# Four expert slabs token tile by token tile, no GpSimd subtractions behind them, and transposes packed two half-chunks to a bank

## The chip, the core and the metric

The kernel runs on one core of a Trainium2 chip. The time is device microseconds of one execution from a measurement of the whole program; lower is better. The engines are TensorE (PE in the profile, its weight loads PEld), VectorE (DVE), ScalarE (ACT), GpSimd (POOL) and SyncE (SP), which issues most of the DMAs.

## The reference, cut to what matters

The program computes two blocks in float32 over 512 tokens of width 1024.

```python
def first_block(x, ...):
    xn = rmsnorm(h, mix_norm_w[l])
    proj = xn @ w_in[l]                    # then pool mixer, gated delta net, gates
    h = h + merged @ w_mix_out[l]
    h = h + peer_ffn(rmsnorm(h, ffn_norm_w[l]), ...)
    return rmsnorm(h, final_norm_w)

def peer_ffn(x, ...):                      # top 16 of 128 x 128 experts per head, 8 heads
    u = jnp.take(expert_down, ei, axis=0)
    act = gelu(einsum("btd,bthkd->bthk", xi, u))
    vv = jnp.take(expert_up, ei, axis=0)
    return einsum("bthk,bthkd->btd", gi * act, vv)

def hybrid_layer(x, norm_pre, w_in, ...):  # block 2
    h = rmsnorm_2(x, norm_pre)
    proj = einsum("bld,de->ble", h, w_in)  # then an SSD scan and stick-breaking attention
```

## The kernel before

**Tiles.** The 512 tokens are four tiles of 128. A float32 product is made of three products of numbers in a shorter format: high times high, high times low, low times high. So each weight slab (128 x 1024) is loaded by SyncE into a raw buffer (fetch), cast on ScalarE to its high half wh, and subtracted from the raw one for its low half wl (emit_part, line 263). The subtraction goes to VectorE where l_dve(i) is true, else to GpSimd. wh and wl have two buffers each. The raw buffers are raw0, raw1 and, during the expert stage, some more (xraw, hraw), which are given up near its end (from nup == NE - 11, only the raw2 list goes round). slab() takes a prepared slab, ahead() prepares the next one and fetches those behind it.

**Transposes.** Activations are turned by TensorE: feat (lines 404 to 413) returns chunk(c, tiles), which makes one transpose per token tile into a PSUM tile tp (two buffers), then split: ScalarE writes the high half (xnh, hnh or x2h), VectorE the low one (xnl, hnl, x2l) from the same PSUM tile. proj_feat calls it for eight chunks of token tiles 0 and 1, then eight chunks of tiles 2 and 3 or in another pairing (sixteen half-chunks), and puts the products of half-chunk s - 2 (first weight slab) and of s - lag (second slab) behind the transposes of half-chunk s. The products write pf. This runs at three places: the start of block 1, of the expert stage and of block 2.

**Expert stage.** 128 down slabs and 128 up slabs are multiplied densely for token tiles 1 to 3; token tile 0 gets its experts by indirect DMAs on GpSimd (gather, ringu and ringv) and sums on VectorE (hn, h_out). The pace of the second gather follows from pace2: `self.pace = (NE * 18 * 512 / 2400 - self.pace2) / (256 - self.ngather)`. An up slab is worked by up(): for t in tiles 1 to 3, six products into y1, y2, y3 (18 in all). The activations come as pairs: pair() loads them, VectorE scales them (wr), and ScalarE and VectorE split that (whl).

**The end of it.** The last two slabs go together: up(*pend, then=add) runs both slabs' tile 1, then tile 2, then tile 3, and after each calls add(t), which adds y into h_out, multiplies by the final norm's weights wf (weigh_tile, hw) and squares for the two norms (square). After the third tile norm_pair(1, 2) gives the norm of token tiles 1 and 2 and writes xs; last_norms() does tiles 0 and 3 beside the first products of block 2. The last slab is converted into the free memory of hnh (self.spare), and from nup == NE - 3 on l_dve is false: all low halves are made on GpSimd. Block 2 (block2_) starts with proj_feat over xs; its third slab is converted into a tile named third.

## Time and profile before

| | us |
|---|---|
| median of 3 runs | 2548.41 (2547.5 to 2549.49) |
| profiled execution | 2550.09 |
| its span, first to last instruction | 2548.3 |
| TensorE busy | 2459.3 (97%) |
| VectorE busy | 1709.0 (67%) |
| ScalarE busy | 994.0 (39%) |
| GpSimd busy | 656.2 (26%) |

A line of the timeline gives start and length in us, engine, line, operation, the tile written <- the tiles read, sizes, how many instructions are put together, and in brackets the idle time of the engine ahead of it and what ended it. A line of windows gives a stretch, its length, the busy time of each engine with instruction counts, the granted TensorE clock (1.00 is 2.4 GHz, 0.50 is 1.2 GHz), the DMA engines' share and GB/s. The page's section 5 groups instructions by line and tile: busy us and mean ns of one, then the idle time ahead of the group and what ended it. All stages are on one clock: block 1 to about 530, the expert stage to 1797.6, block 2 after that.

### The profile page before, as it was taken

To read this page: it belongs to the slowest core of one execution; us is meant where nothing else is said; L and a number is where in the kernel's file an instruction comes from. 1 tells how busy PE (TensorE), PEld (TensorE's weight loads), DVE (VectorE), ACT (ScalarE), POOL (GpSimd) and SP (SyncE) were. 2 spreads that over 40 slices of the span, in tenths; PEclk is the share of its full clock that TensorE was granted. 3 is DMA by queue.
4 is the path that set the end of the run, shared out by engine and by line. 5 is a ranking of instruction groups with operands and counts; after the bars stand their busy time and mean duration, and the time that the engine had idled before them with its cause. 6 is when DMAs were issued, how large, how long until landed. Compare 5 with 4: busy or idle time off the path is not lost.

```text
span 2548.3 us, 34826 instructions
## 1 busy us (share of the span) xinstructions
PE 2459.3 (97%) x13497; PEld 2108.3 (83%) x13497; DVE 1709.0 (67%) x3123; ACT 994.0 (39%) x1453; POOL 656.2 (26%) x401
## 2 busy tenths in 40 slices
PE   6999999989989999999999999999799999999997
PEld 5888788888989999999888888888678988776787
DVE  6776776558998988987577777777754430455433
ACT  4532522332245546455333333333432342444432
POOL 0000000014652222322232323322335234311142
PEclk9999999999999999999999999999899999999999
DMA  3231231324778989889999999998222123222122
GB/s 116 73 93 59 77 110 50 125 101 131 245 269 295 339 286 346 317 315 360 347 326 345 334 343 340 338 323 276 78 67 67 59 91 99 78 60 63 50 91 92
DMA packets 184982, 482.41 MB, mean 189 GB/s; under 512 B 26992, under 2 KB 77296, under 8 KB 184816
## 3 DMA queue, kind: packets, MB, share of 16 engines
q1 hardware_dynamic: 143856, 342.80, 39.5%
q0 software_dynamic: 36864, 134.23, 14.6%
q10 hardware_dynamic: 4096, 3.15, 0.6%
q8 instruction: 106, 1.74, 0.3%
q14 instruction: 60, 0.49, 0.1%
HBM read 422.45 MB, written 53.48 MB: 187 GB/s over the span
## 4 chain that ended last, share of the span: by engine, by line
PE 86%; DVE 11%; issue 2%; ACT 1%; DMA 1%; POOL 0%; SPq 0%; ACTq 0%; DVEq 0%; POOLq 0%
PE pf L175 27%; PE y L175 20%; PE pa L175 18%; PE pt L175 7%; PE psb L175 5%; DVE hn L74 3%; PE pg L175 2%; DVE wl L74 1%; PE tp L180 1%; PE pd L175 1%; PE pyd L175 1%; PE pz L175 1%; DVE oh L74 1%; DVE rt L74 0%; DVE h_out L74 0%
## 5 line engine op out<-in xcount | busy, mean ns | idle before, releaser
L74 ACT CAST wh<-raw 128x1024 fp32r<-128x1024 f32 x310 | 326.4, 1053 | 681.1 <-PE pf L175 303.3
L273 POOL TENSOR_TENSOR wl<-raw,wh 128x1024 fp32r<-128x1024 f32 x113 | 275.9, 2442 | 1047.7 <-ACT wh L74 1029.2
L175 PE MATMUL y<-wh,whl 128*128 128x512 f32 x1524 | 418.0, 395 | 3.9 <-ACT whl L74 3.9
L74 DVE TENSOR_TENSOR wl<-raw,wh 128x1024 fp32r<-128x1024 f32 x197 | 240.9, 1224 | 181.7 <-ACT wh L74 181.6
L175 PE MATMUL pa<-hnh,wl 128*128 128x384 f32 x1024 | 345.2, 337 | 11.0 <-DVE wl L74 5.5
L175 PE MATMUL pa<-hnh,wh 128*128 128x384 f32 x1024 | 347.6, 340 | 3.1 <-ACT st L74 3.1
L175 PEld LDWEIGHTS y<-wh,whl 128*128 128x128 f32 x1524 | 287.4, 189 | 72.3 <-ACT whl L74 4.3
L175 PE MATMUL pa<-hnl,wh 128*128 128x384 f32 x1024 | 343.4, 335 | 0.0
L1480 POOL DMA_INDIRECT ringv<-up,eid x128 | 171.1, 1337 | 422.6 <-DVE h_out L74 388.1
L1480 POOL DMA_INDIRECT ringu<-down,eid x128 | 156.3, 1221 | 355.4 <-DVE hn L74 335.2
L175 PE MATMUL y<-wl,whl 128*128 128x512 f32 x762 | 240.3, 396 | 0.0
L175 PEld LDWEIGHTS pa<-hnh,wl 128*128 128x128 f32 x1024 | 192.7, 188 | 15.7 <-DVE wl L74 7.8
L175 PEld LDWEIGHTS pa<-hnh,wh 128*128 128x128 f32 x1024 | 192.7, 188 | 3.5 <-ACT st L74 3.4
L175 PEld LDWEIGHTS pa<-hnl,wh 128*128 128x128 f32 x1024 | 192.8, 188 | 0.0
L175 PE MATMUL pf<-xnh,wh 128*128 128x512 f32 (+1 forms) x432 | 176.3, 409 | 2.6 <-DVE cy L74 1.7
L74 DVE SCALAR_TENSOR_TENSOR hn<-ringu,hn 128x1024 f32<-128x1024 f32 x128 | 175.0, 1367 | 0.0
L175 PEld LDWEIGHTS y<-wl,whl 128*128 128x128 f32 x762 | 143.6, 189 | 34.7 <-DVE wl L74 0.7
L175 PE MATMUL pf<-x2h,wh 128*128 128x512 f32 (+1 forms) x424 | 169.1, 399 | 2.9 <-DVE cy L74 1.2
L175 PE MATMUL pf<-xnh,wl 128*128 128x512 f32 (+1 forms) x432 | 167.8, 388 | 0.0
L74 DVE SCALAR_TENSOR_TENSOR h_out<-ringv,wgt,h_out 128x1024 f32<-128x1024 f32 x128 | 166.6, 1301 | 0.0
L175 PE MATMUL pf<-xnl,wh 128*128 128x512 f32 (+1 forms) x432 | 166.2, 385 | 0.0
L175 PE MATMUL pf<-x2h,wl 128*128 128x512 f32 (+1 forms) x424 | 166.0, 391 | 0.0
(464 smaller groups left out, 4799.6 us busy)
## 6 DMA issues: line engine op xcount, KB each, us to landing
raw<-w_in_t SPq DMA_DIRECT2D x104, 512.0 KB
raw<-down_t SPq DMA_DIRECT2D x82, 512.0 KB
raw<-up_t SPq DMA_DIRECT2D x55, 512.0 KB
hn<-up_t SPq DMA_DIRECT2D x49, 512.0 KB
Ad<-st SPq DMA_DIRECT2D x32, 768.0 KB
Gd<-stg SPq DMA_DIRECT2D x48, 512.0 KB
ar<-Ad SPq DMA_DIRECT2D x32, 768.0 KB
gr<-Gd SPq DMA_DIRECT2D x32, 768.0 KB
```

The source lines that it names most:

```text
L74: return f(*args, **kw)
L175: self.nc.tensor.matmul(ps, l, r, **kw)
L180: self.nc.tensor.transpose(ps, src, ident)
L273: low = lambda: eng.tensor_tensor(l, raw, h.bitcast(F32), OP.subtract)
L1480: nc.gpsimd.indirect_dma_start(out=(ru, rv)[kind][:, s % 4, :], out_offset=None, in_=a[("down", "up")[kind]], in_offset=bass.IndirectOffse ...
```

## The change

It has four parts.

- The last four up slabs (124 to 127) go through up() together, tile by tile; slabs 126 and 127 are converted into hnh. With four slabs there are places between the slabs of the third tile, and add(2, j) uses them: at the first one it converts block 2's first slab, runs norm_pair(1, 2) and only then the slab's low half, at the second one it converts the second slab.
- l_dve stays true to the end, and weigh_tile always runs on VectorE.
- feat puts the transposes of two half-chunks into one PSUM tile tp of shape [128, 4, 128], a new one for every second half-chunk.
- pace2 goes from 1 to 17.

```diff
-        self.pace, self.pace2, self.gpace = 4.2, 1.0, 4.0
+        self.pace, self.pace2, self.gpace = 4.2, 17.0, 4.0
...
-        if self.spare:
-            (h, l), self.spare = self.spare, None
+        if i in self.spare:
+            h, l = self.spare.pop(i)
...
-            ps = (pool or self.pmm).tile([128, 512], F32, name=self.nm("tp"), tag="tp", bufs=2)
-            for t in tiles:
-                self.tr(ps[:, t * 128:(t + 1) * 128], src[:, t, c * 128:(c + 1) * 128], self.ident)
+            n = len(tiles)
+            if c * n % NT == 0:
+                self.tps = (pool or self.pmm).tile([128, NT, 128], F32, name=self.nm("tp"), tag="tp", bufs=2)
+            o = c * n % NT
+            ps = self.tps[:, o:o + n]
+            for j, t in enumerate(tiles):
+                self.tr(ps[:, j], src[:, t, c * 128:(c + 1) * 128], self.ident)
...
                         if t == 2 and j < n - 1:
-                            self.part(self.cur + 1)
+                            then(t, j)
...
-                if self.nup == NE - 3:
+                if self.nup == NE - 4:
...
-                    self.l_dve = lambda i: False
...
-            for i in range(0, NE - 2, 2):
+            for i in range(0, NE - 4, 2):
                 two, pend = pend, pair(i + 2)
                 up(two[0])
-                if i == NE - 4:
-
-                    self.spare = [hnh[:, 2 * k:2 * k + 2, :].rearrange("p c t -> p (c t)") for k in range(2)]
-                    self.part(self.cur + 2)
+                if i == NE - 6:
+
+                    for j in range(2):
+                        self.spare[self.cur + 3 + j] = [hnh[:, 4 * j + 2 * k:4 * j + 2 * k + 2, :].rearrange("p c t -> p (c t)")
+                                                        for k in range(2)]
+                    self.part(self.cur + 3)
                 up(two[1])
-            self.part(self.cur + 2)
+            self.part(self.cur + 3)
+            last = pend + pair(NE - 2)
             self.drain(gather[0])
...
-            self.weigh_tile(0, nc.gpsimd)
-
+            self.weigh_tile(0)
             self.square(0, 0)
 
-            def add(t):
+            def add(t, j=None):
+
+                if j == 0:
+                    self.late_low = []
+                    self.part(self.cur)
+                    self.all(self.norm_pair(1, 2))
+                    for low in self.late_low:
+                        low()
+                    self.late_low = None
+                elif j == 1:
+                    self.part(self.cur + 1)
+                if j is not None:
+                    return
...
-                self.weigh_tile(t + 1, nc.gpsimd if t == 2 else nc.vector)
+                self.weigh_tile(t + 1)
...
-                    self.all(self.norm_pair(1, 2))
                     self.prep = [self.last_norms()]
-            up(*pend, then=add)
+            up(*last, then=add)
...
-            self.spare = third[:, 0], third[:, 1]
+            self.spare[self.cur + 2] = third[:, 0], third[:, 1]
```

ScalarE at the last expert slabs. Before (raw0 and raw1 are the two raw buffers, hnh is the spare memory for the last slab, whl the split activations):

```order
L74 CAST wh_1704_14851<-raw0_65 128x1024 [waits DMAHW0_49,PE_49,Activation_49]
L74 CAST wh_1706_14876<-raw1_66 128x1024 [waits DMAHW1_49,PE_49,Activation_49]
L74 CAST whl_1709_14882<-wr_1708_14881 128x768 [waits DVE_49]
L74 CAST wh_1710_14905<-raw0_65 128x1024 [waits DMAHW2_49,PE_49,Activation_49]
L74 CAST hnh_4444<-raw1_66 128x1024 [waits DMAHW3_49]
L74 CAST wh_1712_14933<-raw0_65 128x1024 [waits DMAHW4_49,PE_49,Activation_49]
L74 ACTIVATE xs_14939,ss2_67<-h_out_3649 128x1024 [waits DMASW4_49,DMASW2_49,DMASW6_49,DMASW0_49,DVE_49]
```

After, from slab 122 on:

```order
L74 CAST wh_1682_14787<-raw0_65 128x1024 [waits DMAHW4_49,PE_49,Activation_49]
L74 CAST wh_1684_14811<-raw1_66 128x1024 [waits DMAHW7_49,PE_49,Activation_49]
L74 CAST whl_1687_14817<-wr_1686_14816 128x768 [waits DVE_49]
L74 CAST wh_1688_14840<-raw0_65 128x1024 [waits DMAHW0_49,PE_49,Activation_49]
L74 CAST hnh_4436<-raw0_65 128x1024 [waits DMAHW2_49]
L74 CAST wh_1690_14865<-raw1_66 128x1024 [waits DMAHW1_49,PE_49,Activation_49]
L74 CAST hnh_4436<-raw0_65 128x1024 [waits DMAHW3_49]
L74 CAST whl_1693_14875<-wr_1692_14874 128x768 [waits DVE_49]
```

Slabs 126 and 127 are both cast into hnh, from raw0, around the cast of slab 125 from raw1, and the activations of slabs 126 and 127 (the last whl) come behind all four casts.

VectorE at the same place. Before, from slab 125 on:

```order
L74 TENSOR_TENSOR wl_1707_14877<-raw1_66,wh_1706_14876 128x1024 [waits DMAHW1_49,Activation_49]
L74 TENSOR_TENSOR wr_1708_14881<-ar_10866,gr_10867 128x12x2x32
L74 TENSOR_TENSOR whl_1709_14882<-wr_1708_14881,whl_1709_14882 128x768 [waits PE_49,Activation_49]
L74 SCALAR_TENSOR_TENSOR h_out_3649<-ringv_5228,wgt_648_5230,h_out_3649 128x1024 [waits DMASW5_49]
L74 TENSOR_TENSOR wl_1711_14906<-raw0_65,wh_1710_14905 128x1024 [waits DMAHW2_49,Activation_49]
L74 SCALAR_TENSOR_TENSOR h_out_3649<-ringv_5228,wgt_648_5230,h_out_3649 128x1024 [waits DMASW6_49,DVE_49]
L74 SCALAR_TENSOR_TENSOR h_out_3649<-ringv_5228,wgt_648_5230,h_out_3649 128x1024 [waits DMASW7_49,DVE_49]
L74 TENSOR_TENSOR h_out_3649<-h_out_3649,y1_11412 128x1024 [waits PE_49]
```

After, from slab 124 on:

```order
L74 TENSOR_TENSOR wl_1689_14841<-raw0_65,wh_1688_14840 128x1024 [waits DMAHW0_49,Activation_49]
L74 TENSOR_TENSOR hnh_4436<-raw0_65,hnh_4436 128x1024 [waits DMAHW2_49,Activation_49]
L74 TENSOR_TENSOR wl_1691_14866<-raw1_66,wh_1690_14865 128x1024 [waits DMAHW1_49,Activation_49]
L74 TENSOR_TENSOR hnh_4436<-raw0_65,hnh_4436 128x1024 [waits DMAHW3_49,Activation_49]
L74 TENSOR_TENSOR wr_1692_14874<-ar_10850,gr_10851 128x12x2x32 [waits DVE_49]
L74 TENSOR_TENSOR whl_1693_14875<-wr_1692_14874,whl_1693_14875 128x768 [waits PE_49,Activation_49]
L74 TENSOR_TENSOR hw_14879<-h_out_3641,rawx_4430 128x1024 [waits DMAHW5_49]
L74 TENSOR_TENSOR h_out_3641<-h_out_3641,y1_11396 128x1024 [waits PE_49]
L74 TENSOR_TENSOR hw_14879<-h_out_3641,rawx_4430 128x1024 [waits DVE_49]
L74 TENSOR_TENSOR h_out_3641<-h_out_3641,y2_11397 128x1024 [waits PE_49]
L74 TENSOR_TENSOR hw_14879<-h_out_3641,rawx_4430 128x1024 [waits DVE_49]
L74 TENSOR_SCALAR v1_68<-ss2_67 128x2 [waits Activation_49]
```

The four slabs' subtractions stand in the order 124, 126, 125, 127, then wr and whl of the last pair; the chain of norm_pair (v1 is its first step) now stands behind the second addition of y in place of the third.

TensorE at the start of block 2. Before (each tp number is a PSUM tile of its own):

```order
L180 MATMUL tp_1722_15048<-ident_60,xs_14939 128x128 x2
L180 MATMUL tp_1723_15054<-ident_60,xs_14939 128x128 [waits DVE_49]
L180 MATMUL tp_1723_15054<-ident_60,xs_14939 128x128
L175 MATMUL pf_1719_15041<-x2h_15031,wl_1713_14934 128x256 [waits Activation_49,Pool_49]
L175 MATMUL pf_1719_15041<-x2l_15032,wh_1712_14933 128x256
L175 MATMUL pf_1719_15041<-x2h_15031,wh_1712_14933 128x256
L180 MATMUL tp_1724_15062<-ident_60,xs_14939 128x128 [waits DVE_49]
L180 MATMUL tp_1724_15062<-ident_60,xs_14939 128x128
```

After:

```order
L180 MATMUL tp_1704_15035<-ident_60,xs_14880 128x128 x2
L175 MATMUL pf_1701_15023<-x2h_15013,wl_1695_14946 128x256 [waits Activation_49]
L175 MATMUL pf_1701_15023<-x2l_15014,wh_1694_14945 128x256
L175 MATMUL pf_1701_15023<-x2h_15013,wh_1694_14945 128x256
L180 MATMUL tp_1704_15035<-ident_60,xs_14880 128x128 [waits DVE_49]
L180 MATMUL tp_1704_15035<-ident_60,xs_14880 128x128
L175 MATMUL pf_1701_15023<-x2h_15013,wl_1695_14946 128x256 [waits Activation_49]
L175 MATMUL pf_1701_15023<-x2l_15014,wh_1694_14945 128x256
L175 MATMUL pf_1701_15023<-x2h_15013,wh_1694_14945 128x256
L180 MATMUL tp_1707_15055<-ident_60,xs_14880 128x128 [waits PE_49]
```

Each tp number now takes two half-chunks, four transposes. The first half-chunk of a bank has lost its wait for VectorE, and the second one has a wait for VectorE, for the x2l that reads the first half of the same bank.

## Rows read from the trace of the kernel before

**Rows 1.** Page, section 1: each engine's busy us, share and instructions.

```profile
PE 2459.3 (97%) x13497; PEld 2108.3 (83%) x13497; DVE 1709.0 (67%) x3123; ACT 994.0 (39%) x1453; POOL 656.2 (26%) x401
```

**Rows 2.** Timeline of PE, block 1's first pass (start us, us, instruction).

```profile
17.77 0.44 PE L180 MATMUL tp<-ident,x_t 128*128 128x128 f32 x2
...
18.63 0.44 PE L180 MATMUL tp<-ident,x_t 128*128 128x128 f32 x2
```

**Rows 3.** Timeline of PE, start of the expert stage.

```profile
540.26 0.69 PE L180 MATMUL tp<-ident,hn 128*128 128x128 f32 x2 [0.87 <-DVE hnl L74]
...
548.82 0.44 PE L180 MATMUL tp<-ident,hn 128*128 128x128 f32 x2 [3.00 <-DVE hnl L74]
```

**Rows 4.** Timeline of PE, the seam and the start of block 2.

```profile
1808.91 1.26 PE L180 MATMUL tp<-ident,xs 128*128 128x128 f32 x4 [11.32 <-DVE xs L74]
...
1811.96 0.63 PE L180 MATMUL tp<-ident,xs 128*128 128x128 f32 x2
...
1820.24 0.38 PE L180 MATMUL tp<-ident,xs 128*128 128x128 f32 x2
...
1821.17 0.38 PE L180 MATMUL tp<-ident,xs 128*128 128x128 f32 x2
...
1839.58 1.73 PE L180 MATMUL ptb<-ident,bc 128*128 128x128 f32 x8 [4.27 <-issue]
...
1865.64 1.05 PE L175 MATMUL pgr<-triu,gw 128*48 128x128 f32 x8 [1.98 <-DVE gw L74]
```

**Rows 5.** Timeline of DVE, the last slabs and the seam.

```profile
1778.71 1.22 DVE L74 TENSOR_TENSOR wl<-raw,wh 128x1024 fp32r<-128x1024 f32 x1
...
1783.15 0.95 DVE L74 TENSOR_TENSOR wr<-ar,gr 128x768 f32<-128x768 f32 x1
...
1802.30 0.16 DVE L74 SCALAR_TENSOR_TENSOR rt<-rt,me 128x2 f32<-128x2 f32 x1
1802.49 2.21 DVE L74 SCALAR_TENSOR_TENSOR rs<-rt,rs 128x2 f32<-128x2 f32 x1
...
1813.13 0.48 DVE L74 SCALAR_TENSOR_TENSOR x2l<-tp,vec,x2h 128x256 fp32r<-128x256 f32 x1 [0.53 <-ACT x2h L74]
...
1821.17 0.48 DVE L74 SCALAR_TENSOR_TENSOR x2l<-tp,vec,x2h 128x256 fp32r<-128x256 f32 x1 [0.44 <-ACT x2h L74]
```

**Rows 6.** Timeline of POOL, the seam.

```profile
1802.33 2.35 POOL L273 TENSOR_TENSOR wl<-raw,wh 128x1024 fp32r<-128x1024 f32 x1 [3.39 <-issue]
```

**Rows 7.** Windows: length, busy us by engine, clock, DMA share, GB/s (header left out).

```profile
1764.00:1780.24 16.24, 16.24 (x72) 13.16 (x71) 12.67 (x13) 5.86 (x6) 4.73 (x5) 1.00 0.66 226
1808.90:1816.20 7.30, 6.63 (x29) 6.03 (x30) 4.02 (x16) 4.41 (x10) 0.00 (x0) 0.50 0.00 0
1816.20:1821.00 4.80, 3.40 (x28) 3.03 (x27) 3.26 (x10) 1.38 (x4) 0.00 (x0) 1.00 0.00 0
1907.00:2040.00 133.00, 133.00 (x976) 118.95 (x975) 58.17 (x123) 44.38 (x97) 56.77 (x30) 1.00 0.20 64
```

**Rows 8.** Timeline of ACT, the last slabs and the seam.

```profile
1786.63 1.06 ACT L74 CAST hnh<-raw 128x1024 fp32r<-128x1024 f32 x1 [0.47 <-DMA raw<-up_t]
...
1809.78 0.90 ACT L74 ACTIVATE x2h<-tp,vec 128x256 fp32r<-128x256 f32 x2 [0.57 <-PE tp L180]
...
1820.66 0.47 ACT L74 ACTIVATE x2h<-tp,vec 128x256 fp32r<-128x256 f32 x1 [0.45 <-PE tp L180]
```

**Rows 9.** Timeline of SyncE's queue, two raw loads.

```profile
1779.96 0.33 SPq L247 DMA_DIRECT2D raw<-up_t  x1
...
1783.26 0.33 SPq L247 DMA_DIRECT2D raw<-up_t  x1
```

**Rows 10.** Page, section 5: the subtractions on GpSimd and on VectorE.

```profile
L273 POOL TENSOR_TENSOR wl<-raw,wh 128x1024 fp32r<-128x1024 f32 x113 | 275.9, 2442 | 1047.7 <-ACT wh L74 1029.2
...
L74 DVE TENSOR_TENSOR wl<-raw,wh 128x1024 fp32r<-128x1024 f32 x197 | 240.9, 1224 | 181.7 <-ACT wh L74 181.6
```

**Rows 11.** Timeline of DVE, block 2, the chain ahead of pgr.

```profile
1859.26 2.40 DVE L74 TENSOR_SCALAR sp<-sp 128x64 f32<-128x64 f32 x1
```

More of the change, by code (lines that the diff above doesn't have):

```diff
@@ L103, in __init__ @@
         self.pending, self.prep, self.convs = None, [], []
-        self.pace, self.pace2, self.gpace = 4.2, 1.0, 4.0
+        self.pace, self.pace2, self.gpace = 4.2, 17.0, 4.0
         self.rpace, self.space, self.routed = 3.4, 2.2, 0
-        self.l_dve, self.spare = (lambda i: True), None
+        self.l_dve, self.spare = (lambda i: True), {}
     def nm(self, s):
@@ L1755, in block2_, with weigh_tile @@
                 self.proj_tok("w_out_t", i, (mh, ml), put_o(i), tag=(("mm", 2), ("sc", 4))[i % 2], last=(i == 3))
-    def weigh_tile(self, t, eng=None):
-        (eng or self.nc.vector).tensor_tensor(self.hw[:, t, :], self.h[:, t, :], self.wf, OP.mult)
+    def weigh_tile(self, t):
+        self.nc.vector.tensor_tensor(self.hw[:, t, :], self.h[:, t, :], self.wf, OP.mult)
     def square(self, k, t, vector=False):
```

2 lines of the change are left out of this document (1 added, 1 removed).

## The prediction

> **What bounds the kernel now.** I read the busy table first: TensorE is busy 97% of the span, VectorE 67%, ScalarE 39%, GpSimd 26% [rows 1]. So every microsecond has to come out of TensorE's few idle stretches, and whatever the change adds costs time only where it opens a new one. Next I read TensorE's rows at the three places where the transposes named tp stand: the start of block 1, of the expert stage and of block 2 [rows 2 to 4]. The widest gap near the edit is the seam: the first transpose of block 2 comes at 1808.91 after 11.32 us of idleness [rows 4]. VectorE fills it with the additions h_out<-h_out,y, their hw products and then a norm chain of fourteen tiny steps, one of which takes 2.21 us where its neighbour takes 0.16 [rows 5]; a GpSimd subtraction lies on exactly that one [rows 6]. Last, the table by stretches: after the gap TensorE has granted clock 0.50 (1.2 GHz) until 1816.2, then 1.00 (2.4 GHz) [rows 7].
>
> **The change part by part.** All times below are on the clock of the profiled execution of before.
>
> *Packed transposes.* Before, every half-chunk (two token tiles) has a PSUM bank of its own, and there are two. Its transposes wait for the x2l of the half-chunk two back. After, an even half-chunk and the following odd one share a bank; the built order makes the odd one's transposes wait for VectorE's x2l of the even one just ahead. That chain is in the rows: transposes at 1820.24, ScalarE's x2h at 1820.66 [rows 4, 8], VectorE's x2l at 1821.17 for 0.48, so it ends at 1821.65 [rows 5]. An odd half-chunk therefore starts no sooner than 1.41, with the handover some 1.45 us, after the even one. Before, neighbours start 0.93 apart with two weight slabs (1820.24 to 1821.17 [rows 4]) and 0.86 with one (17.77 to 18.63 [rows 2]). The even one needs no wait any more, but its earlier start is capped by the products in front of it. So a pair takes 1.45 + 0.93 in place of 1.86 (+0.52), or 1.45 + 0.86 in place of 1.72 (+0.59). At the lower clock the chain is longer, 1811.96 to 1813.61, 1.65 to 1.70 us [rows 4, 5], but so are the products beside it; I take +0.6 there too. A place has eight pairs, four in the first pass over token tiles 0 and 1 with one slab, four in the second with two. The first pair of each place is cheaper (+0.3), because there the third half-chunk waits already, 0.87 us in the expert stage [rows 3]. Block 1: 0.3 + 3 x 0.6 + 4 x 0.52 = **+4.2**. Expert stage: **+4.2**. Block 2: again 4.2, and one subtraction more, that of the slab named third, stands among VectorE's x2l: 1.22 by VectorE's row of its kind [rows 5]; it pushes the x2l behind it by up to that, and the norm steps of the first pass, which the packing sets between the two x2l of a pair, by up to as much again: 2.2 of 2.4, since TensorE has nothing else there, so **+6.4** (bounds 3 and 9). Bounds of each place: 0, if what the odd half waits for is over already when TensorE gets there, and 8, if the new idleness brings the 0.50 clock. After 16.2 TensorE was busy only 3.40 of 4.80 us and kept 1.00 [rows 7], so I stay with the small figures.
>
> These rows already bear out one rule. The Trainium skill (PSUM — Partial Sum Buffer, "PSUM bank collisions raise a hardware error") says that TensorE writing and another engine reading the same bank must be kept apart, whichever columns they touch. It is a rule against this packing: by it the wait cannot be dropped, and the three places cost 14.8 us; were columns enough, they would cost 0 to 2.
>
> *Four last slabs tile by tile.* The order shows six raw loads with only two buffers: slabs 124 and 126 and 127 all use raw0, 125 uses raw1. A load can start when the subtraction of its predecessor is through: wl ends at 1779.93, the load is issued at 1779.96; the next is issued at 1783.26 and a cast waits for it to the end, until 1786.63 [rows 5, 8, 9]: 3.35 us from issue to use. Token tile 1 now wants all four slabs within 4 x 6 x 0.232 = 5.57 us (72 records in 16.24 us in which TensorE never rests, those at the edges counted in part [rows 7]). Slab 123 ends with that stretch, at 1780.24, and slab 124's part of tile 1 near 1781.63. Slab 126 is loaded at 1783.3, cast by 1784.4 (1.05), subtracted by 1785.6 (1.22); slab 125's cast and subtraction stand behind those two, at 1785.4 and 1786.8. TensorE waits 3.8 us for the first and 0.95 for the second, and ends slab 125 near 1787.8. Slab 127 can only be issued at 1785.65: loaded 1789.0, cast 1790.05, subtracted 1791.3; behind it on VectorE is wr (0.95 [rows 5]), and then on ScalarE the cast of whl (0.83, an estimate from 768 of 1024 columns of the 1.06 us cast), without which slab 126 cannot run: 1793.1, so TensorE waits another 5.35. Tile 1 ends near 1795.9, tile 2 at 1801.5, tile 3 at 1807.1. These are new idle stretches of about 10 us. After the seam's idle stretch of before the granted clock is 0.50 for 7.3 us [rows 7], which costs at most half of that; for the shorter new ones I take 1.7 in all (0 to 3.6).
>
> What follows is the norm of tiles 1 and 2, which now needs only tile 2: addition and hw 1.22 each (as wl, of the same shape [rows 5]), the square of hw on ScalarE 1.25 (a pass as long as the 1.06 of the cast [rows 8], and the reading of its sum), fourteen small steps 2.8 (0.16 and the handover each, no longer inflated), xs 1.15, and 0.3 of handovers: 7.9 us after tile 2. VectorE then does two subtractions, the second behind a cast (2.2 where xs hides a part), then the addition of tile 3 (1.2), and ScalarE squares that (1.25) and hw beside it before the first x2h (another 1.1): 13.65 us after tile 2. So the first x2h starts at 1801.55 + 1.7 + 13.65 = 1816.9, where before it started at 1809.78 [rows 8]: **+7.1**. With no raw wait tile 2 would end at 1780.24 + 11.1 = 1791.4 and x2h start at 1805.05: -4.7. These are the ends; the upper one is +10, with both clock penalties.
>
> *No GpSimd subtractions in block 2.* Some 94 subtractions of 2442 ns leave GpSimd for VectorE at 1224 ns [rows 10]. VectorE has room: between 1907 and 2040, for one, it is busy 58 of 133 us, with TensorE busy through [rows 7]. I count them at nothing where TensorE never waits; what hides them is that VectorE runs ahead of the slab it prepares, and without that cover each would show 1.22. In the wait of 4.27 us ahead of ptb [rows 4] the engine waited for is VectorE (its chain cy, ws2hl, cy, r, h_out, bc), and two subtractions fall into that: between 0 and 2 x 1.22, less what GpSimd's company cost the chain before; I take the middle, **+1.2**. In the chain ahead of pgr a step sp on 128x64 elements took 2.40, longer than a subtraction of 128x1024, and TensorE waited 1.98 [rows 4, 11]: that goes, **-2** (bounds -6 and +5 for the rest of block 2).
>
> *The second gather's pace.* Its additions come some 17 us sooner and thereby denser. In the up slabs VectorE is busy 12.67 of 16.24 us with TensorE busy throughout [rows 7]: 0.
>
> **Sum.** 4.2 + 4.2 + 7.1 + 6.4 + 1.2 - 2 = +21.1 on an execution of 2550.09, so 2571.2. The execution lies 1.7 above the median of 2548.41, and the forecast for the median is 2570.
>
> **The rivals.** *A, it works as meant (faster).* One mechanism: the norm of tiles 1 and 2 comes early, because the raw loads keep up. Price -4.7 at the seam; with packing free, +1.2 - 2 in the rest and no subtractions lost, the sum is -5.5, 2543. It decides if slab 126's load lands before 1781.6. Against it: the load has to wait for the subtraction that ends at 1779.93. For it: only that the 3.35 us were read beside gathers that are done sooner now. *B, the raw wait is as I say, the packing is hidden* under waits of the norm's xs and x_t that are there anyway: 7.1 + 1.2 - 2 + 1.2 = +7.5, 2556. For it: TensorE waits 3.00 us in the middle of the expert stage's place anyway [rows 3]. *C, the packing costs what I say, the raw wait does not come* because the loads are quicker: 4.2 + 4.2 - 4.7 + 6.4 + 1.2 - 2 = +9.3, 2558. *D, the clock stays at 0.50 through the serialised halves*: then the four two-slab pairs of a place take 1.70 and the products of a half-chunk at the low level, 2 x 0.93, in place of 2.38: 1.2 more each and 4.8 less what waits hide, 4.3: 3 x 4.3 = +13, 2583. *E, VectorE's order binds in block 2*: subtractions wait there for casts of ScalarE with the scan's work queued behind: +8, 2578.
>
> **How the numbers follow.** My forecast has 0.48, A 0.04, B 0.14, C 0.14, D 0.09, E 0.11. Range 2555 to 2583: it takes in B, C and E and stops at D's edge. A measurement here can tell about 0.2% (5 us) from no change. Faster is A, 0.04; same is a mild form of B or C with one more saving, 0.05; slower 0.91.
>
> **What would show it.** Right: TensorE's y rows of tile 1 with two gaps of 4 to 5 us, released by ScalarE's hnh or whl and behind them a DMA; odd tp rows released by x2l, with pairs 2.3 to 2.4 us long; no GpSimd rows at 2.4 us after the expert stage; the first x2h some 7 us later against the last slab 123 y. Wrong: y rows without a gap, tp rows evenly 0.9 apart, or new waits for wl in the middle of block 2.

## The result, and the profile after

The changed kernel takes **2575.35 us** (median of four executions, 2571.83 to 2580.35), where the kernel before takes 2547.95 beside it: a ratio of 1.0105, interval 1.0093 to 1.0117 (the ratios here are those of the measurement; the quotient of two medians can differ from them by some 0.1%). The profiled execution takes 2571.83, its span 2570.0; it is the quickest of the four. The forecast was 2570, with a range of 2555 to 2583 and slower as the likely side.

The page's first section of the kernel after answers to [rows 1]. VectorE has gained 78 us and GpSimd has lost 231; TensorE has gained 5 us with the same number of instructions. The other 16 us or so of the longer span are idle time of TensorE.

```profile
PE 2464.6 (96%) x13497; PEld 2112.2 (82%) x13497; DVE 1787.4 (70%) x3218; ACT 994.1 (39%) x1453; POOL 425.5 (17%) x306
```

The timeline of PE of the kernel after, start of the expert stage, answers to [rows 3] (start us, length us, instruction, in brackets the idle time ahead and what ended it):

```profile
543.28 0.69 PE L180 MATMUL tp<-ident,hn 128*128 128x128 f32 x2 [0.45 <-DVE hnl L74]
...
546.12 0.69 PE L180 MATMUL tp<-ident,hn 128*128 128x128 f32 x2 [0.44 <-DVE hnl L74]
...
557.37 0.44 PE L180 MATMUL tp<-ident,hn 128*128 128x128 f32 x2
...
559.83 0.44 PE L180 MATMUL tp<-ident,hn 128*128 128x128 f32 x2 [0.38 <-DVE hnl L74]
```

Now the second half-chunk of each bank waits for VectorE's hnl, the reader of the bank's first half; the first half-chunk of the next bank follows without a wait. From one second half-chunk to the next, a pair, it is 2.84 us in the first rows (543.28 to 546.12) and 2.46 in the last (557.37 to 559.83; the row at 557.37 has come to its turn without a wait).

The timeline of PE of the kernel after, from the last four slabs to block 2, answers to [rows 4]:

```profile
1791.44 0.73 PE L175 MATMUL y<-wh,whl 128*128 128x512 f32 x2 [3.30 <-ACT wh L74]
1792.89 1.22 PE L175 MATMUL y<-wl,whl 128*128 128x512 f32 x2 [0.72 <-DVE wl L74]
...
1799.35 4.77 PE L175 MATMUL y<-hnh,whl 128*128 128x512 f32 x12 [4.39 <-ACT whl L74]
...
1820.66 0.69 PE L180 MATMUL tp<-ident,xs 128*128 128x128 f32 x2 [5.38 <-DVE h_out L74]
1823.76 1.11 PE L180 MATMUL tp<-ident,xs 128*128 128x128 f32 x4 [2.41 <-DVE x2l L74]
...
1860.13 1.94 PE L180 MATMUL ptb<-ident,bc 128*128 128x128 f32 x8 [5.46 <-issue]
...
1888.28 0.59 PE L175 MATMUL pf<-x2h,wh 128*128 128x512 f32 x1 [2.15 <-DVE cy L74]
...
2196.96 0.47 PE L175 MATMUL pf<-x2h,wh 128*128 128x512 f32 x1 [2.86 <-DVE merged L74]
...
2508.93 0.36 PE L175 MATMUL pt<-wh,m2l 128*128 128x256 f32 x1 [2.90 <-DVE sg L74]
```

The first three rows are new: TensorE waits in the middle of token tile 1. The gap of 11.32 us is gone, in its place stand 5.38 and 2.41. The wait ahead of ptb has grown from 4.27 to 5.46; pgr's 1.98 us is gone, but half of that has come back in the wait behind it, for cy: 2.15, where the kernel before has 1.19. The last two rows stand late in block 2, where the kernel before has 0.85 us of idle time at either.

The timelines of ACT and then of DVE of the kernel after, at the last four slabs and the seam, answer to [rows 5, 8]:

```profile
1789.39 1.04 ACT L74 CAST hnh<-raw 128x1024 fp32r<-128x1024 f32 x1 [5.70 <-DMA raw<-up_t]
1790.35 1.04 ACT L74 CAST wh<-raw 128x1024 fp32r<-128x1024 f32 x1
1795.26 1.04 ACT L74 CAST hnh<-raw 128x1024 fp32r<-128x1024 f32 x1 [3.88 <-DMA raw<-up_t]
1798.47 0.83 ACT L74 CAST whl<-wr 128x768 fp32r<-128x768 f32 x1 [2.16 <-DVE wr L74]
...
1822.73 0.45 ACT L74 ACTIVATE x2h<-tp,vec 128x256 fp32r<-128x256 f32 x1
```

```profile
1790.47 1.22 DVE L74 TENSOR_TENSOR hnh<-raw,hnh 128x1024 fp32r<-128x1024 f32 x1 [4.64 <-ACT hnh L74]
...
1797.48 0.95 DVE L74 TENSOR_TENSOR wr<-ar,gr 128x768 f32<-128x768 f32 x1
```

This is the chain that the prediction wrote down from the order. ScalarE's cast of slab 126 (1789.39) waits 5.70 us for the DMA; the cast of slab 125 (1790.35), whose raw slab has long been there, stands behind it, and TensorE's first new gap ends with it at 1791.44. The cast of slab 127 waits another 3.88 us for its DMA; wr (1797.48) and the cast of whl (1798.47) stand behind, and they end TensorE's third gap at 1799.35.

Following single matmuls through both traces gives a ledger of how far the kernel after lags behind the kernel before, in us, in the profiled executions:

| place | lag | step | predicted step |
|---|---|---|---|
| behind block 1's transposes | 5.07 | +5.07 | +4.2 |
| ahead of the expert stage | 0.83 | -4.24 | 0 |
| behind the expert stage's transposes | 5.97 | +5.14 | +4.2 |
| end of slab 123 | 5.89 | -0.08 | 0 |
| first x2h of block 2 (1809.78, 1822.73) | 12.95 | +7.06 | +7.1 |
| ptb (1839.58, 1860.13) | 20.55 | +7.60 | +6.4 + 1.2 |
| end | 21.78 | +1.23 | -2 |
| sum | | +21.78 | +21.1 |

### The profile page after: what moved, and what is told of

Read it like the earlier page. It is cut to its first block, busy times and chain, and to the rows that moved or that the text cites. A ratio compares the mean times of both kernels' runs of the same rounds, so it can differ in the third digit from the quotient of the medians.

```text
span 2570.0 us, 34808 instructions
## 1 busy us (share of the span) xinstructions
PE 2464.6 (96%) x13497; PEld 2112.2 (82%) x13497; DVE 1787.4 (70%) x3218; ACT 994.1 (39%) x1453; POOL 425.5 (17%) x306
## 4 chain that ended last, share of the span: by engine, by line
PE 85%; DVE 10%; issue 2%; ACT 2%; DMA 1%; POOL 0%; SPq 0%; ACTq 0%; DVEq 0%; POOLq 0%
PE pf L175 27%; PE y L175 20%; PE pa L175 17%; PE pt L175 7%; PE psb L175 5%; DVE hn L74 3%; PE pg L175 2%; DVE wl L74 1%; PE tp L180 1%; PE pyd L175 1%; PE pd L175 1%; PE pz L175 1%; DVE oh L74 1%; ACT wh L74 0%; DVE cy L74 0%
## 5 line engine op out<-in xcount | busy, mean ns | idle before, releaser
L74 DVE TENSOR_TENSOR wl<-raw,wh 128x1024 fp32r<-128x1024 f32 x287 | 351.1, 1224 | 364.3 <-ACT wh L74 363.3
L74 DVE SCALAR_TENSOR_TENSOR h_out<-ringv,wgt,h_out 128x1024 f32<-128x1024 f32 x128 | 164.4, 1285 | 0.0
L175 PE MATMUL pf<-x2l,wh 128*128 128x512 f32 (+1 forms) x424 | 163.6, 386 | 0.0
```

The costliest lines, as they stand in the source:

```text
L74: return f(*args, **kw)
L175: self.nc.tensor.matmul(ps, l, r, **kw)
```

## The experiments

All ratios are to the kernel before, run in turn on the same chip; its medians there were 2549.37, 2549.36, 2549.42 and 2548.42. Medians with the number of executions:

| kernel | us | n | ratio | interval |
|---|---|---|---|---|
| pack_only | 2565.94 | 4 | 1.0057 | 1.0041 to 1.0074 |
| nopack | 2559.99 | 5 | 1.0038 | 1.0024 to 1.0052 |
| dve | 2553.32 | 10 | 1.0017 | 1.0008 to 1.0027 |
| early | 2554.02 | 10 | 1.0020 | 1.0010 to 1.0030 |
| altpack | 2561.68 | 4 | 1.0048 | 1.0032 to 1.0065 |
| early2 | 2551.86 | 9 | 1.0011 | 1.0000 to 1.0022 |
| sel | 2548.37 | 10 | 0.9996 | 0.9987 to 1.0006 |
| best | 2548.86 | 10 | 0.9999 | 0.9990 to 1.0009 |
| best2 | 2549.56 | 12 | 1.0004 | 0.9994 to 1.0014 |
| pace | 2549.25 | 10 | 0.9999 | 0.9990 to 1.0008 |
| quiet | 2543.80 | 11 | 0.9981 | 0.9972 to 0.9990 |
| after_again | 2579.21 | 4 | 1.0126 | 1.0110 to 1.0143 |

Costs in us below are differences of medians; the intervals say how sure they are (for pack_only 16.6 by the medians, 10 to 19 by the interval).

The theory was the prediction's own sum: packing costs at all three places, the raw loads cost at the seam, the subtractions little. The rivals were B (packing is hidden), C (the raw wait does not come) and E (VectorE's order binds in block 2).

### The packing alone, and everything but the packing

pack_only is the kernel before with only this edit; nopack is the kernel after with this edit undone.

```diff
-            ps = (pool or self.pmm).tile([128, 512], F32, ..., tag="tp", bufs=2)
-            for t in tiles:
-                self.tr(ps[:, t * 128:(t + 1) * 128], src[:, t, ...], self.ident)
+            n = len(tiles)
+            if c * n % NT == 0:
+                self.tps = (pool or self.pmm).tile([128, NT, 128], F32, ..., tag="tp", bufs=2)
+            o = c * n % NT
+            ps = self.tps[:, o:o + n]
+            for j, t in enumerate(tiles):
+                self.tr(ps[:, j], src[:, t, ...], self.ident)
```

> The kernel before with the packed transposes alone. My theory (the odd half-chunk waits for the x2l of the even one in the same bank): the rows of tp at the three places show a wait released by xnl, hnl or x2l in front of every second half-chunk, pairs are 2.3 to 2.5 us long with two slabs in place of 1.86, and the product rows behind each place come 4 to 6 us later against the place's start; in all +12 to +15, less what the clock gives back, 2555 to 2563. Rival B (hidden under waits that are there anyway): under 2 us at each place, 2549 to 2553.

> The changed kernel without the packing, each half-chunk again in its own bank. My theory: the three places go back to the spacing of before (0.93 us with two slabs), the two idle stretches of tile 1 stay (3.3 and 4.4 us, released by ScalarE's wh and whl), the seam's x2h stays 7 us late: 2555 to 2562. Rival (the packing is harmless and the seam and the subtractions carry the loss): 2570 or more.

Measured: packing alone costs 16.6 us, the rest alone 10.6; together 27.2, and the whole change 27.4 by its own comparison (30.8 when repeated). So the two halves add up within the spread of their executions, and both B and C are out; pack_only lies above the 2555 to 2563 that I had expected. pack_only's lag rises by 5.13 in block 1, by 5.2 at the start of the expert stage and by 6.3 in block 2, 5.9 of it between the first x2h and ptb; these three are 16.6. The other 5.2 us of its profiled lag of 21.8 come later in the expert stage (3.8 between 840 and 1030, 1.5 between 1255 and 1776) in an execution that is its slowest, 2571.86. About 2 of the 3.8 stand behind a wait of 2.08 us at 923.17 (1.75 in the kernel before), after which the granted clock is 0.50 for 3.4 us where the kernel before keeps 1.00; the rest is not assigned.

The timeline of PE of nopack shows the raw waits without any packing:

```profile
1785.69 0.74 PE L175 MATMUL y<-wh,whl 128*128 128x512 f32 x2 [3.37 <-ACT wh L74]
...
1793.73 4.76 PE L175 MATMUL y<-hnh,whl 128*128 128x512 f32 x12 [4.59 <-ACT whl L74]
```

They are the gaps of the kernel after (3.30 and 4.39; the short one between them, 0.72, is here 0.71), with the packing undone.

### Two half-chunks to a bank, but not neighbours

altpack keeps two half-chunks in each bank but puts the even ones into one bank and the odd ones into the other (against the kernel after):

```diff
-            if c * n % NT == 0:
-                self.tps = (pool or self.pmm).tile(...)
-            o = c * n % NT
-            ps = self.tps[:, o:o + n]
+            if n == NT or c % 4 == 0:
+                self.tps = [(pool or self.pmm).tile(...) for _ in range(NT // n)]
+            o = 0 if n == NT else c % 4 // 2 * n
+            ps = self.tps[0 if n == NT else c % 2][:, o:o + n]
```

> The changed kernel with the same packing, two half-chunks of four transposes in one bank, but with neighbours in different banks: half-chunks 0 and 2 share one bank, 1 and 3 the other. Everything else as changed. My theory (what costs is that a half-chunk follows its own bank neighbour at once): the waits at tp go back to those of before, spacing 0.93 us with two slabs, and the time is that of nopack, 2556 to 2564. Rival (the packed tile itself costs, by the form of its transposes or of the split behind them): 2570 or more.

Measured: 2561.68, beside nopack's 2559.99; by the intervals the two are not told apart. The timeline of PE of altpack at the expert stage:

```profile
539.12 0.69 PE L180 MATMUL tp<-ident,hn 128*128 128x128 f32 x2 [0.86 <-DVE hnl L74]
...
547.69 0.44 PE L180 MATMUL tp<-ident,hn 128*128 128x128 f32 x2 [3.00 <-DVE hnl L74]
```

These are the gaps of the kernel before (0.87 and 3.00 in [rows 3]). So it is not the shared bank that costs, but that a half-chunk follows its own bank neighbour: then the transposes, the cast, the subtraction and the next transposes run one behind the other. With the other bank in between, that chain lies beside TensorE's next half-chunk, as before. The Trainium skill (PSUM — Partial Sum Buffer, "PSUM bank collisions raise a hardware error") keeps TensorE's writes and another engine's reads of one bank apart. The 16.6 us of pack_only are what that separation costs here when bank neighbours follow each other; with the other bank in between it costs nothing that these runs can tell (altpack is 1.7 above nopack). No run here lets the two overlap.

### The low halves on VectorE alone

dve is the kernel before with this edit (pace, packing and slabs as before):

```diff
-                    self.l_dve = lambda i: False
...
-            self.weigh_tile(0, nc.gpsimd)
+            self.weigh_tile(0)
...
-                self.weigh_tile(t + 1, nc.gpsimd if t == 2 else nc.vector)
+                self.weigh_tile(t + 1)
```

> The kernel before with all low halves and hw products of block 2 on VectorE, nothing else. My theory: the seam's idle stretch of 11.3 us loses the two steps of 2.2 us that GpSimd holds up and a little of the hw products, 4 us; the wait ahead of pgr goes (2.0); the wait ahead of ptb grows by 1.2: 2541 to 2546. Rival E (VectorE's order binds in block 2): new waits for wl there, 2551 to 2556.

Measured: +4, rival E's range and not mine. The timeline of PE and two rows of DVE:

```profile
1809.91 1.26 PE L180 MATMUL tp<-ident,xs 128*128 128x128 f32 x4 [13.12 <-DVE xs L74]
...
2178.95 0.47 PE L175 MATMUL pf<-x2h,wh 128*128 128x512 f32 x1 [2.86 <-DVE merged L74]
...
2490.91 0.36 PE L175 MATMUL pt<-wh,m2l 128*128 128x256 f32 x1 [2.90 <-DVE sg L74]
...
1802.85 1.23 DVE L74 TENSOR_TENSOR wl<-raw,wh 128x1024 fp32r<-128x1024 f32 x1 [2.21 <-ACT wh L74]
...
1805.24 1.23 DVE L74 TENSOR_TENSOR hw<-h_out,rawx 128x1024 f32<-128x1024 f32 x1
```

Where I expected a gain at the seam, the gap grew from 11.32 to 13.12: the steps of the norm run at 0.16 us again, but a subtraction (1802.85, which waits 2.21 for its cast) and the last hw product (1805.24) now stand in VectorE's own order ahead of the norm. And the two gaps late in block 2 are there (2.86 and 2.90): they come from the subtractions and from nothing else in the change.

### The last loads earlier

early gives slabs 123, 124 and 126 memory of their own (the free hnl and hnh) and begins the last slabs' parts sooner; early2 gives it to slabs 122, 123, 126 and 127. Against nopack, early2's core:

```diff
-                if i == NE - 6:
-                    for j in range(2):
-                        self.spare[self.cur + 3 + j] = [hnh[...] ...]
-                    self.part(self.cur + 3)
...
+                    n = i + k - (NE - 9)
+                    if 0 <= n < 4:
+                        t, m = ((hnl, 0), (hnl, 4), (hnh, 0), (hnh, 4))[n]
+                        m2 = self.cur + 2 + 2 * (n > 1)
+                        if n == 2:
+                            self.part(m2 - 1)
+                        self.spare[m2] = [t[...] ...]
+                        self.part(m2)
+                        if n == 1:
+                            self.part(m2 + 1)
+                        self.ahead(False)
```

> As nopack, but slabs 123, 124 and 126 are converted into the memory of hnl and hnh, one or two slabs earlier, so that the raw loads of 124 to 127 are not strung on one buffer behind the end of slab 123. My theory: y of tiles 1 to 3 runs without the two idle stretches, tile 2 ends 10 us earlier, the first x2h some 12 us earlier than in nopack, and the time is 2543 to 2550. Rival (the wait is not the raw buffer's but that of the order of casts and subtractions, or VectorE's): the stretches stay at 6 us or more, 2555 to 2562.

> As early, with four slabs (122, 123, 126, 127) converted ahead into hnl and hnh, one slab earlier, so that the cast of the last pair's activations no longer stands behind the casts of slabs 126 and 127. My theory: the 3.7 us wait for whl in tile 1 goes, tile 2 ends 4 to 5 us earlier than in early, the first transposes of block 2 too: 2546 to 2552, with the block 2 losses of the subtractions still in it. Rival (the wait for whl hangs on its own two buffers or on VectorE's scaling): the stretch stays over 2 us, 2551 to 2556.

Measured: early -6.0 against nopack, less than I had expected, early2 -8.1. The timelines of PE and of ACT of early:

```profile
1787.59 2.20 PE L175 MATMUL y<-hnh,whl 128*128 128x512 f32 x6 [3.72 <-ACT whl L74]
...
1783.44 1.05 ACT L74 CAST wh<-raw 128x1024 fp32r<-128x1024 f32 x1 [1.80 <-DMA raw<-up_t]
1786.71 0.83 ACT L74 CAST whl<-wr 128x768 fp32r<-128x768 f32 x1 [2.21 <-DVE wr L74]
```

The first gap has nearly gone (0.34 us are left), but 3.72 us stay: the cast of the last whl (1786.71) stands behind the cast of slab 127 (1783.44), which waits 1.80 for its DMA, and behind VectorE's wr. early2 has two gaps of 2.0, both ended by whl. So the loads, with the order of casts behind them, were the cause of most of what nopack lost at the seam, but each remedy leaves a piece of it in another place of ScalarE's order.

### Some low halves back on GpSimd

sel is early2 with five subtractions given back (numbers count slabs from the stage's last ones on):

```diff
+                    p0 = self.cur
+                    self.l_dve = lambda i: i - p0 not in (3, 4, 6, 53, 85)
```

> As early2, but five of block 2's low halves go back to GpSimd: the two in the chain ahead of ptb, one ahead of the next cy, one ahead of merged and one ahead of the last sg. My theory (each of these stands on VectorE in front of a step that TensorE waits for): the idle stretches go back from 5.5 to 4.3, 2.9 to 0.9 and 2.9 to 0.9 us, in all 4 to 6 us less than early2. Rival (the subtractions on VectorE are free there, the difference is the granted clock's): same as early2 within 2 us.

Measured: -3.5 against early2, a little under the 4 to 6 expected. The timeline of PE of sel:

```profile
1838.95 1.37 PE L180 MATMUL ptb<-ident,bc 128*128 128x128 f32 x8 [4.27 <-issue]
...
1865.05 1.04 PE L175 MATMUL pgr<-triu,gw 128*48 128x128 f32 x8 [1.97 <-DVE gw L74]
...
2174.29 0.50 PE L175 MATMUL pf<-x2h,wh 128*128 128x512 f32 x1 [0.85 <-DVE merged L74]
...
2487.35 0.39 PE L175 MATMUL pt<-wh,m2l 128*128 128x256 f32 x1 [0.85 <-DVE sg L74]
```

ptb is back at 4.27, the two late gaps at 0.85 each, and pgr's 1.97 is back too, with the wait for cy behind it at 1.20 in place of early2's 2.13: -1.2, -2.0, -2.0, +2.0 and -0.9, in all -4.1; the difference of 0.6 to the medians is not assigned. The subtractions on VectorE cost by where they stand in its order, not by their sum.

### Two versions meant to gain

best puts the first low half, the last hw and its squares behind the last addition, which the first transposes of block 2 wait for, and gives the second slab's low half to GpSimd (against sel); best2 does the like with that low half on VectorE, behind the first x2l, and with the last slabs' parts begun in another order. best's core:

```diff
-                    for low in self.late_low:
-                        low()
-                    self.late_low = None
-                elif j == 1:
-                    self.part(self.cur + 1)
+                    self.lows, self.late_low = self.late_low, None
...
+                if t == 2:
+                    for low in self.lows:
+                        low()
+                    self.weigh_tile(3)
+                    def late():
+                        self.square(0, 3)
+                        yield
+                        self.square(1, 0)
+                        yield
+                        yield from self.last_norms()
+                    self.prep = [late()]
```

> As sel, and at the seam the addition of y of the last tile stands on VectorE ahead of the first slab's low half, the squares of the last tile stand on ScalarE behind the first two x2h, and the second slab's low half goes to GpSimd. My theory: the first transposes of block 2 come 2 to 3 us earlier, 2539 to 2545, below the kernel before. Rival (the norms of tiles 0 and 3 are then late and the gain comes back as a wait in the second pass): the wait for xs there grows by 2 us, 2543 to 2548.

> As sel, with slabs 125 and 126 converted behind the activations of slabs 124 and 125, and at the seam, on VectorE, the addition of y of the last tile ahead of the first slab's low half and the second slab's low half behind the first two x2l (all on VectorE, so nothing of GpSimd's lies beside them), the squares of the last tile on ScalarE behind the first two x2h. My theory: the two waits for whl (2.1 and 0.5 us in sel) go, the first transposes come 2 to 4 us earlier, without the 4.2 us gap of best behind them: 2542 to 2546, below the kernel before by 0.1 to 0.3%. Rival (what is won at the seam is lost again to the wait for xs in the second pass or to the granted clock): 2547 to 2550.

Neither gained on sel: 2548.86 and 2549.56, both above what I had expected. best2 does not test its idea, though. It leaves out that the raw buffer of block 2's second slab must not be refilled before its low half is made, and its time is touched by that, as its timelines of DVE and PE show:

```profile
1810.53 1.23 DVE L74 TENSOR_TENSOR wl<-raw,wh 128x1024 fp32r<-128x1024 f32 x1 [3.00 <-DMA raw<-w_in_t]
...
1812.21 0.69 PE L180 MATMUL tp<-ident,xs 128*128 128x128 f32 x2 [2.62 <-DVE x2l L74]
```

The subtraction waits 3.00 us for the refill, the x2l stand behind it, and TensorE waits 2.62 for them. What best2 would take with the right order is not shown. The timelines of PE, DVE and POOL of best:

```profile
1805.92 0.66 PE L180 MATMUL tp<-ident,xs 128*128 128x128 f32 x4 [2.74 <-DVE h_out L74]
1810.74 0.69 PE L180 MATMUL tp<-ident,xs 128*128 128x128 f32 x2 [4.17 <-DVE x2l L74]
...
1806.92 3.38 DVE L74 TENSOR_TENSOR hw<-h_out,rawx 128x1024 f32<-128x1024 f32 x1
...
1806.26 2.95 POOL L273 TENSOR_TENSOR wl<-raw,wh 128x1024 fp32r<-128x1024 f32 x1 [41.16 <-ACT wh L74]
```

The first transposes come sooner, but the hw product beside GpSimd's subtraction takes 3.38 us instead of 1.22, and TensorE then waits 4.17 for the x2l behind it: the gain is given back one step later. The product ends at 1810.30, 1.09 us behind the subtraction's end at 1809.21, nearly its own length, as if it had got hardly anything done until then. The Trainium skill (SBUF — State Buffer, "Who interferes with whom") says that a VectorE instruction with two SBUF inputs contends with a GpSimd instruction that reads SBUF; the trace agrees, with 3.38 against 1.22. Of VectorE's two-port modes the same section says that whoever issues first gets the shared ports for the whole instruction; the 1.09 us fit that here too, for an instruction with two inputs.

### The pace alone

```diff
-        self.pace, self.pace2, self.gpace = 4.2, 1.0, 4.0
+        self.pace, self.pace2, self.gpace = 4.2, 17.0, 4.0
```

> The kernel before with pace2 = 17 alone. My theory: the second gather's additions come earlier, TensorE stays busy through the up slabs, no change: 2547 to 2551. Rival (the denser additions delay a low half or the transfers of raw slabs): new idle stretches between 1260 and 1780, 2552 or more.

Measured: no difference (0.9999, 0.9990 to 1.0008), and no new idle stretch between 1260 and 1780.

### A version that gains

quiet is the kernel before with the seam cleared of GpSimd: the hw products of token tiles 0 and 3 go to VectorE behind the norm, a square moves out of the way, the second slab's part waits, and only five slabs' subtractions are on VectorE.

```diff
-                        if t == 2 and j < n - 1:
-                            self.part(self.cur + 1)
...
-            self.weigh_tile(0, nc.gpsimd)
+            p0 = self.cur + 2
...
-                self.weigh_tile(t + 1, nc.gpsimd if t == 2 else nc.vector)
+                if t < 2:
+                    self.weigh_tile(t + 1)
...
-                    self.square(1, 0)
                     self.all(self.norm_pair(1, 2))
-                    self.prep = [self.last_norms()]
+                    self.weigh_tile(0)
+                    self.weigh_tile(3)
+                    def late():
+                        self.square(1, 0)
+                        yield from self.last_norms()
+                    self.prep = [late()]
+                    self.l_dve = lambda i: i - p0 in (1, 5, 6, 7, 8)
```

> The kernel before with its two last slabs, its banks and its pace, and only the GpSimd work taken off the steps that TensorE waits for: at the seam the hw products of token tiles 0 and 3 and the second slab's low half go to VectorE behind the norm of tiles 1 and 2, in block 2 four low halves (near pgr and the transposes of xsf) go to VectorE, all others stay on GpSimd. My theory: VectorE's two norm steps of 2.2 us are 0.2 us, its hw products 1.2 in place of 2.2 and 2.6, the seam's idle stretch loses 3 to 5 us, and the stretches ahead of pgr and xsf 3 us, with those ahead of ptb, merged and sg as before: 2541 to 2545. Rival (the three passes that move to VectorE hold up the first x2l by as much as the norm gains): the second gap of the seam grows to 3 us or more, 2545 to 2549.

Measured: 2543.80, 0.9981 (0.9972 to 0.9990) of the kernel before, and the quickest of all. Its timelines of PE and of DVE:

```profile
1803.33 1.27 PE L180 MATMUL tp<-ident,xs 128*128 128x128 f32 x4 [6.29 <-DVE xs L74]
1807.04 0.69 PE L180 MATMUL tp<-ident,xs 128*128 128x128 f32 x2 [2.44 <-DVE x2l L74]
...
1863.90 0.50 PE L175 MATMUL pf<-x2h,wh 128*128 128x512 f32 x1 [2.15 <-DVE cy L74]
...
1802.24 0.16 DVE L74 SCALAR_TENSOR_TENSOR rs<-rt,rs 128x2 f32<-128x2 f32 x1
```

The step rs, 2.21 us in [rows 5], takes 0.16; the gap ahead of the first transpose is 6.29 in place of 11.32. Three rows of VectorE make up that 5.03: rs, the step behind it (2.26 before, 0.16 now) and an hw product (2.15 before, 1.23 now). Some of it comes back as 2.44 behind the first transposes. By ptb the kernel leads by 3.5 us. Behind it pgr's gap is gone, with 2.15 in place of 1.19 at cy (1863.90), and a wait of 0.78 for xsf too; the lead is then 6.6, and it keeps that to the end.

### The kernel after again

> The changed kernel once more, beside the kernel before on the same chip and in more executions. My theory: packing (16.6 over before when alone) and the rest (10.6 when alone) add up, 2573 to 2579, and the executions differ by 5 to 9 us among themselves with the granted clock, with the same idle stretches in the profile. Rival (the first four executions were unlucky): 2568 to 2572.

The kernel after once more, unchanged, measured 2579.21 in this comparison (four executions, 2575.62 to 2585.36), 3.9 above the first, and ends 4.5 us later in the profiled execution. The idle stretches are nearly the same; what differs most is the granted clock behind them, shown in the last section.

## Why the prediction was right, and where its steps were off

**The side and the mechanism** held: forecast 2570, measured 2575.35, slower; the profiled execution came to +21.7 where the sum said +21.1. That these two agree so closely is in part luck, as the ledger shows: 4.2 us of what the packing cost in block 1 were made up by the clock before the expert stage. Without that the sum of the steps is 26.0, nearer to what the medians say (+27.4, and +30.8 when repeated).

**Packing**: right in place and in mechanism, mis-sized. I had 4.2 at the start of block 1 and of the expert stage; 5.07 and 5.14 were measured. The term that was mis-sized is the lower clock, for which I took the same +0.6 a pair as at the full one (1.45 + 0.86 = 2.31 in the first pass, 1.45 + 0.93 = 2.38 in the second). Windows of the expert stage's place, the kernel before and then the kernel after, from the first transpose to the same product behind the last one, then of two stretches of it in the kernel after (length, busy time of PE, PEld, DVE, ACT and POOL, granted clock, DMA share, GB/s):

```profile
538.70:561.80 23.10, 19.07 (x129) 17.90 (x130) 14.20 (x36) 10.27 (x22) 4.61 (x2) 0.85 0.35 129
539.50:567.80 28.30, 21.27 (x129) 19.44 (x130) 14.56 (x37) 10.41 (x22) 4.43 (x2) 0.76 0.29 101
543.20:546.10 2.90, 2.40 (x10) 2.10 (x10) 2.14 (x12) 0.95 (x2) 0.00 (x0) 0.50 0.99 401
557.30:562.30 5.00, 4.25 (x35) 3.77 (x33) 1.95 (x5) 1.90 (x4) 0.00 (x0) 1.00 0.01 3
```

The place is 5.2 us longer (5.14 by single matmuls): 3.0 of that is idle time of TensorE (28.30 - 21.27 against 23.10 - 19.07), and 2.2 is that the same matmuls take longer. A mean clock of 0.76 over 28.30 us is 13.6 us at 0.50, one of 0.85 over 23.10 some 6.9. So the idle time is less than my 4.2, and the rest is clock: a pair takes 2.46 at 1.00, close to the 2.38, and 2.84 at 0.50, and the place runs at 0.50 for twice as long, which the +4.2 left out. Rival D's mechanism was there for a part of each place, though not for all of it.

At block 2 the 6.4 held as a sum (7.60 with ptb's 1.2), but not in its parts. From the first x2h to ptb the kernel before takes 29.80, pack_only 35.66: the packing alone cost 5.9, with the subtraction of third still on GpSimd. In nopack that subtraction is on VectorE, and from the first x2h to the last product of third it takes 25.56 in place of 25.14. The sum had 4.2 for the packing and 2.2 for the norm steps that it moves and for the subtraction, about half each. So the packing with the norm steps cost 5.9 in place of 5.3 and the subtraction some 0.5 in place of 1.1; that the sum came out is in part luck.

**The raw loads at the seam**: +7.06 measured against +7.1, but four parts of it were off and cancelled, which is luck too. The idle gaps are 8.41 us in place of 10.1 (3.30 for 3.8, 0.72 for 0.95, 4.39 for 5.35). Tile 1 takes 1803.96 - 1786.58 = 17.38 us, of which 5.57 are products at the full clock, so the clock took 3.4, where I had chosen 1.7 and had an upper end of 3.6. Slab 124 begins at 1786.58, 0.45 later than I read it off the window. And from the end of tile 2 (1809.54) to the first x2h it took 13.19 in place of 13.65: -1.7 + 1.7 + 0.45 - 0.46 = 0. The upper end of +10 does not follow from its terms: 3.6 in place of 1.7 gives +9.0.

**Subtractions on VectorE in block 2**: this is the step that failed. I had -2 for the rest, from pgr's gap; that gap went, but +1.23 came out. The first loss is next to it: the wait for cy grew by 0.96. The others stand late in block 2. The timeline of PE of the kernel before at the two places:

```profile
2177.06 0.50 PE L175 MATMUL pf<-x2h,wh 128*128 128x512 f32 x1 [0.85 <-DVE merged L74]
...
2488.60 0.38 PE L175 MATMUL pt<-wh,m2l 128*128 128x256 f32 x1 [0.85 <-DVE sg L74]
```

The timelines of ACT and DVE of the kernel after, ahead of the row at 2508.93:

```profile
2505.88 1.04 ACT L74 CAST wh<-raw 128x1024 fp32r<-128x1024 f32 x1 [3.81 <-issue]
...
2506.96 1.23 DVE L74 TENSOR_TENSOR wl<-raw,wh 128x1024 fp32r<-128x1024 f32 x1 [4.21 <-ACT wh L74]
2508.10 0.68 DVE L74 SCALAR_TENSOR_TENSOR sg<-sg,pf 128x512 f32<-128x512 f32 x1
```

ScalarE's cast ends at 2506.92; the subtraction starts with it, 4.21 us after VectorE's last work, takes 1.23, and only then comes sg, which TensorE waits for. On GpSimd the same subtraction stood in nobody's way: there it starts at 2488.73, behind the start of sg at 2487.86. That is rival E's mechanism, at two places (merged and sg), each about 2.0 us of idle time: 2.86 - 0.85 and 2.90 - 0.85. In the lag it shows as +0.4 at merged and +3.5 at sg, because the granted clock differs there too: the kernel before is at 0.50 from 2195.1 to 2198.5, where the kernel after keeps 1.00, and the kernel after is at 0.50 from 2509.7 to 2513.1, where the kernel before keeps 1.00. dve shows both without any other part of the change, sel shows them gone when five subtractions go back. I had counted the subtractions "at nothing where TensorE never waits"; but TensorE did wait at these two, 0.85 us each, and the prediction left out rows as short as that.

**The seam with VectorE alone**, as expected for dve: wrong. I counted the inflated norm steps as a gain and not the subtraction and product that come into the chain in their place; +1.8 for -4. The prediction had also seen only one inflated step of the norm; there are two (2.21, and 2.26 behind it).

**The pace**: 0, as said.

**The rivals**: A did not happen: the load of slab 126 is issued at 1785.86, behind the subtraction that ends at 1785.83, as the trace of before had told. B is refuted by pack_only (+16.6), C by nopack, whose gaps are those of the kernel after. D was there in part, E at two places.

## What to carry to other kernels

Two results in one PSUM bank cost nothing that could be told here when another bank's work ran between them, and the full chain of producer and readers when they were neighbours: if banks are to be packed, interleave. When a cheap operation is moved to an engine on the critical chain, look at its own input: what costs is not its length but that the engine stands waiting for that input with the chain's next step behind it, so look at every place at which the bottleneck waits for that engine, the waits under a microsecond too. Before a stage is rebuilt around its end, see whether the raw loads can come as fast as the new order wants them; here two buffers could not, and a smaller edit (GpSimd kept out of the norm) gained 4.6 us.

## What the runs showed that was not expected

**The same idle stretch can be followed by either clock.** Windows just behind an idle stretch of 2.31 us that ends in the same matmul in three kernels; the columns are length, busy time of PE, PEld, DVE, ACT and POOL, granted clock, DMA share and GB/s. The kernel before, pack_only, the kernel after, and after_again:

```profile
62.10:66.00 3.90, 3.90 (x11) 2.98 (x12) 0.23 (x2) 3.63 (x16) 0.00 (x0) 0.50 0.22 87
67.20:71.10 3.90, 3.88 (x11) 2.96 (x12) 0.28 (x2) 3.58 (x16) 0.00 (x0) 0.50 0.18 74
67.20:71.10 3.90, 3.90 (x19) 2.75 (x20) 0.23 (x2) 3.63 (x16) 0.00 (x0) 1.00 0.15 61
67.20:71.10 3.90, 3.90 (x13) 2.94 (x14) 0.16 (x3) 3.71 (x16) 0.00 (x0) 0.58 0.18 75
```

The kernel before and pack_only come out of it at 0.50, the kernel after at 1.00, after_again at 0.58 on the average of the stretch. TensorE is busy throughout in each. This is where the kernel after made up 2.9 us of its lag in its profiled execution; another 1.1 followed at 240, behind 1.88 us of idleness. The edit cannot be given credit: after_again is the same program. Executions of the kernel after differ by 8 to 10 us (2571.83 to 2580.35, 2575.62 to 2585.36), those of the kernel before beside after_again by 5.2 (2546.56 to 2551.79), in the other comparisons, with 20 to 24 executions, by 7.9 to 9.3, and those of quiet by 3.2 (2541.78 to 2545.01). So a wider spread of the changed kernel is not shown.

**How much a GpSimd subtraction holds VectorE up.** 0.16 to 2.21 us for a step on 128x2 [rows 5], 0.20 (the kernel after) to 2.40 for a step on 128x64 [rows 11], 1.22 to 3.38 for the product in best. The step on 128x2 starts at 1802.49, behind GpSimd's start at 1802.33, and ends at 1804.70, GpSimd's subtraction at 1804.68 [rows 5, 6]. The next step, 2.26 us long, lies beside GpSimd's hw product (1804.64, 2.33 long). So a tiny step can cost as much as the whole of GpSimd's pass.

**A slow drift.** Between 1285 and 1776 the lag behind the kernel before grows by 1.1 us in after_again (8.1 to 9.2) and by 0.8 in pack_only, and shrinks by 0.8 in the first execution of the kernel after, with TensorE busy all but 0.2 us and the granted clock at 1.00; its cause stays open.
